# Splits of the next weights behind the root of a norm, and loads of the expert output stage behind its weight loads

## The chip, the cores and the metric

The kernel runs on one core of a Trainium2 chip. The metric is the time of one execution in microseconds (us). Work is spread over TensorE (PE in the profile), VectorE (DVE), ScalarE (ACT) and SyncE (SP), which issues the DMAs from HBM. GpSimd does almost nothing here.

## The reference

Two transformer blocks in a row, on one sequence of 256 tokens with a model width of 1024, all in float32. Cut to what matters here:

```python
# block 1
proj = rmsnorm(h, g_mix) @ w_in                       # mLSTM heads and sliding-window attention
h = h + concat([hm, ha]) @ w_out
h = h + memory_cross_attention(rmsnorm(h, g_cross), rmsnorm(mem, g_mem), ...)
h = h + peer_ffn(rmsnorm(h, g_ffn), w_pq, ..., expert_down, expert_up)
x = rmsnorm(h, g_final)
# block 2, two layers: an even mixer, then an odd one, each followed by an FFN
hn = rms_norm(h, mix_norm_g[layer])
h = h + even_mixer(hn, ...)     # q and k of its first half: rms_norm per head of 64
h = h + conv_ffn(rms_norm(h, ffn_norm_g[layer]), ...)

def rmsnorm(x, g):
    return x * lax.rsqrt(jnp.mean(x * x, axis=-1, keepdims=True) + EPS) * g

def peer_ffn(...):   # per token: 8 heads x 16 of 16384 experts
    a = gelu(expert_down[eidx] . x);  out = sum(g * a * expert_up[eidx])
```

## The kernel before, in words

**Matrix products.** Activations lie transposed, features on the partitions. Each product runs in three passes on a high and a low part of both operands (`mm3`, L439 to L441; `out_step`, L577 to L579 for products that are summed into the residual `h`). So a weight of 128x1024 (512 KB) is handled in four steps: SP loads it into `raw` (L417, `weight`), ACT rounds it into `hi` (L429), DVE subtracts to get `lo` (L430, called the split below), and PE runs 24 matmuls of 256 columns, or 12 of 512 columns, with it. I call that work of PE a piece. There are five weight buffers in the first part of block 1, three in the expert part and six in block 2.

**Norms.** A norm does not hold up the product that follows it. The product runs on `h` times the gain, and the factor 1/rms comes in at the end, in what reads the accumulator. `Norm.columns` (L202) sums the squares on PE into a `tp` bank and calls `rsqrt` (L450): ten dependent DVE operations on 128x2 elements, `rs_m` (L453), `rs_g`, `rs_a` twice, `rs_z`, `rs_a` twice, `rs_p` twice, and the root `rs_y` (L468). `rows` (L218) spreads the root along the tokens: transposes on PE (L213), a copy on ACT (L215) into a tile such as `xR`. `tick` counts pieces: the columns come after the first piece, the rows after the third. `Final` (L256) joins the last norm of block 1 with the first of block 2; its `columns` (L289) run the chain twice, the second time on `fq`, and multiply the two roots (L299). In the even mixer q and k get a norm per head (`head_norm`, L1345), which calls the same `rsqrt` on 128x8 elements, once for each half of the tokens; the transposes of q and k (L1379) wait for it.

**The expert part.** For the experts the kernel computes all of them: 128 weights of `down`, whose outputs go through a gelu and are stored in HBM (`store`, 256 KB for each pair of weights, 55 pairs; the rest stays on the chip), while a gating matrix (`ga`, `gb`) is built. Then the expert output stage runs 128 weights of `up`: for each pair `step` (L1228) reloads the activations (`u`, SP, L1239), multiplies the gate in place (`ga`, DVE, L1240), splits the product (L434, L435) and gives it to `out_step`. A ring of three buffers holds the reloads. The residual `h` (1 MB, from `spill`) and the constants of block 2 (`c_late`, 1.09 MB) are loaded by one DMA each as the stage begins.

**Order.** The code is traced once; a scheduler then puts the instructions of every engine into an order by its own estimate of times, and each engine works in that order. `issue_after(x)` adds the condition that an instruction stands behind `x`. The kernel used it at a few places before, through `gate` in `weight`.

Of the kernel before, what the change touches and what calls it, by code (L numbers as in the profile page):

```python
# [150 lines left out]
class Norm:  # L151
# [50 lines left out]
    def columns(self):  # L202
        ps = self.b.tp()
        self.sums(ps, "s", 0)
        self.r2 = self.b.rsqrt(ps[:, :2], 2, 1.0, keep=self.tag)
        self.r = [self.r2[:, t:t + 1] for t in range(2)]
# [49 lines left out]
class Final(Norm):  # L256
# [32 lines left out]
    def columns(self):  # L289
        b, nc = self.b, self.b.nc  # L290
        ps = b.tp()
        self.sums(ps, "s", 0)
        self.sums(ps, "f", 2)
        self.rf = b.rsqrt(ps[:, :2], 2, 1.0, keep="f")
        q = b.sp.tile([P, 2], F32, tag="fq", name="fq")
        nc.vector.tensor_mul(q, ps[:, 2:4], self.rf)
        nc.vector.tensor_mul(q, q, self.rf)
        r = b.rsqrt(q, 2, 1.0, keep=self.tag)
        nc.vector.tensor_mul(r, r, self.rf)  # L299
        self.r2 = r  # L300
        self.r = [r[:, t:t + 1] for t in range(2)]
# [70 lines left out]
class Builder:  # L372
    def __init__(self, tc, nc, A, out, stages=None):
        self.tc, self.nc, self.A, self.out = tc, nc, A, out
        self.stages = stages
        self.flip = 0
        self.gate = None
        self.free = 100
        self.later = []
        self.mark = None  # L380

# [27 lines left out]
    def weight(self, ap, width=D, parts=1):  # L409
# [6 lines left out]
        for c in cuts:  # L416
            nc.sync.dma_start(raw[:, c], ap[:, c])  # L417
        hi = wp.tile([P, D], F32R, tag="hi", name="hi", bufs=bufs)
        lo = wp.tile([P, D], F32R, tag="lo", name="lo", bufs=bufs)
        with ExitStack() as ctx:  # L420
            if self.gate:
# [4 lines left out]
                if self.free < -4:  # L426
                    self.gate = None
            for c in cuts:
# [21 lines left out]
    def rsqrt(self, ss, n, inv, keep=None):  # L450
# [17 lines left out]
        v.tensor_mul(out, p, z)  # L468
# [144 lines left out]
    def consts(self, names, arr):  # L613
        n = sum(CONST_COLS[k] for k in names)
        t = self.cp.tile([P, n], F32, tag=arr, name=arr)
        self.nc.sync.dma_start(t, self.A[arr])
        o = 0
        for k in names:
            self.c[k] = t[:, o:o + CONST_COLS[k]]
            o += CONST_COLS[k]  # L620

# [455 lines left out]
    def peer(self, xu, base, cw, cx, cq, late, spill, nxt):  # L1077
        nc, A = self.nc, self.A
        mm = nc.tensor.matmul
        with ExitStack() as ctx:  # L1080
# [139 lines left out]
            nc.sync.dma_start(self.h, spill)  # L1220
            self.cp = self.pool(late, "c_late", side="right")
            self.consts(LATE, "c_late")
# [4 lines left out]

            def step(n):  # L1228
                j = order[n // 2]
                if n % 2 == 0:  # L1230
                    if j < GA and cg is not None and "x" not in coef:
# [3 lines left out]
                        self.xq = self.pool(late, "xq2", side="right")  # L1235
                    src = gslice(j, 2)
                    if j < kept:
                        a = acts_next()
                        nc.sync.dma_start(a.rearrange("p i t -> p (i t)"), store[j // 2])  # L1239
                        nc.vector.tensor_mul(src, src, a)  # L1240
# [506 lines left out]
```

## Time and profile before

| | |
|---|---|
| median of 3 runs | 1697.31 us (1692.98 to 1709.5) |
| the profiled execution | 1709.04 us, span 1707.3 us |
| PE busy | 1662.3 us, 97% of the span |
| DVE busy | 1262.0 us, 74% |
| ACT busy | 874.4 us, 51% |
| DMA | 318 MB, mean 186 GB/s |

PE is busy for 97% of the span; 45 us of the span are left. The busy time counts matmuls that run at half clock as well, so it hides a second kind of loss. A share of the whole span says little in such a kernel: what matters is where PE stands still, and what it waits for there.

### The profile page before, as it was taken

What the parts mean: (1) busy time and instruction counts of PE and PEld (TensorE: products, weight loads), DVE (VectorE), ACT (ScalarE), POOL (GpSimd) and SP (SyncE); (2) the same over time, 40 slices, a digit from 0 to 9 for tenths busy, and PEclk for the clock granted to TensorE, in tenths of its full rate; (3) what the DMA queues carried; (4) which work ended last, traced back from release to release, by engine and by line L of the source; (5) the groups of instructions that cost most, each with busy time, mean ns of one, the idle gap of its engine ahead of it and who ended that gap; (6) DMA issues with size and microseconds to landing.
All of it is one profiled execution on the core that took longest, in us unless ns stands there. A gap on an engine that the chain in (4) does not pass through costs nothing.

```text
span 1707.3 us, 33027 instructions
## 1 busy us (share of the span) xinstructions
PE 1662.3 (97%) x13220; PEld 1582.3 (93%) x13220; DVE 1262.0 (74%) x2504; ACT 874.4 (51%) x1358; POOL 0.8 (0%) x11
## 2 busy tenths in 40 slices
PE   7999999999999999999999999899999999999999
PEld 7879899999999999988999999688999997699998
DVE  7686669998798985678655555977777784677775
ACT  6445445545555555444444444655555565455553
POOL 0000000000000000000000000000000000000000
PEclk9999999999999999999999999999999999999999
DMA  8433544577555655889655556543556645345652
GB/s 279 141 104 118 172 166 153 191 230 263 183 195 191 199 193 187 287 291 321 205 186 186 186 186 210 188 138 100 170 190 193 197 151 185 112 155 194 197 192 68
DMA packets 97515, 318.02 MB, mean 186 GB/s; under 512 B 11841, under 2 KB 13505, under 8 KB 96850
## 3 DMA queue, kind: packets, MB, share of 16 engines
q1 hardware_dynamic: 89154, 301.39, 54.2%
q10 hardware_dynamic: 8208, 14.52, 2.2%
q8 instruction: 104, 1.70, 0.4%
q14 instruction: 49, 0.40, 0.1%
HBM read 299.36 MB, written 16.52 MB: 185 GB/s over the span
## 4 chain that ended last, share of the span: by engine, by line
PE 83%; DVE 10%; DMA 4%; issue 2%; ACT 1%; SPq 0%; ACTq 0%; DVEq 0%
PE tp L439 11%; PE tp L441 11%; PE tp L440 11%; PE acc L578 10%; PE acc L579 9%; PE acc L577 9%; PE acc L439 5%; PE acc L440 5%; PE acc L441 5%; DVE lo L430 3%; DMA u<-store 2%; PE tp L1188 1%; PE tp L1189 1%; DMA raw<-w_in_t 1%; ACT hi L429 1%
## 5 line engine op out<-in xcount | busy, mean ns | idle before, releaser
L429 ACT ACTIVATE hi<-raw 128x1024 fp32r<-128x1024 f32 (+1 forms) x533 | 560.6, 1058 | 643.8 <-PE tp L440 247.5
L430 DVE TENSOR_TENSOR lo<-raw,hi 128x1024 fp32r<-128x1024 f32 (+1 forms) x533 | 649.0, 1220 | 295.1 <-ACT hi L429 294.8
L439 PE MATMUL tp<-xh,hi 128*128 128x256 f32 x1680 | 473.2, 282 | 0.4 <-ACT u L1203 0.4
L441 PE MATMUL tp<-xh,lo 128*128 128x256 f32 x1680 | 468.2, 279 | 1.8 <-DVE lo L430 1.8
L440 PE MATMUL tp<-xl,hi 128*128 128x256 f32 x1680 | 467.9, 279 | 0.0
L441 PEld LDWEIGHTS tp<-xh,lo 128*128 128x128 f32 x1680 | 316.6, 188 | 2.2 <-DVE lo L430 2.0
L439 PEld LDWEIGHTS tp<-xh,hi 128*128 128x128 f32 x1680 | 316.8, 189 | 0.6 <-ACT u L1203 0.6
L440 PEld LDWEIGHTS tp<-xl,hi 128*128 128x128 f32 x1680 | 317.0, 189 | 0.0
L578 PE MATMUL acc<-u,hi 128*128 128x256 f32 x1024 | 287.6, 281 | 5.2 <-DVE u L435 5.2
L579 PE MATMUL acc<-u,lo 128*128 128x256 f32 x1024 | 287.4, 281 | 2.3 <-DVE lo L430 2.3
L577 PE MATMUL acc<-u,hi 128*128 128x256 f32 x1024 | 287.1, 280 | 0.0
L578 PEld LDWEIGHTS acc<-u,hi 128*128 128x128 f32 x1024 | 195.4, 191 | 6.1 <-DVE u L435 6.1
L579 PEld LDWEIGHTS acc<-u,lo 128*128 128x128 f32 x1024 | 192.7, 188 | 2.9 <-DVE lo L430 2.9
L577 PEld LDWEIGHTS acc<-u,hi 128*128 128x128 f32 x1024 | 192.3, 188 | 0.0
L439 PE MATMUL acc<-hi,xh 128*128 128x512 f32 (+1 forms) x256 | 101.3, 398 | 6.4 <-ACT y L474 5.8
L440 PE MATMUL acc<-lo,xh 128*128 128x512 f32 (+1 forms) x256 | 100.4, 392 | 0.7 <-DVE lo L430 0.7
L441 PE MATMUL acc<-hi,xl 128*128 128x512 f32 (+1 forms) x256 | 100.0, 391 | 0.0
L577 PE MATMUL acc<-uh,hi 128*128 128x256 f32 x352 | 97.3, 277 | 0.1
L578 PE MATMUL acc<-ul,hi 128*128 128x256 f32 x352 | 97.3, 277 | 0.0
L579 PE MATMUL acc<-uh,lo 128*128 128x256 f32 x352 | 97.1, 276 | 0.0
L577 PE MATMUL acc<-oh,hi 128*128 128x256 f32 x256 | 72.7, 284 | 0.0
L578 PE MATMUL acc<-ol,hi 128*128 128x256 f32 x256 | 71.8, 280 | 0.0
(433 smaller groups left out, 2673.6 us busy)
## 6 DMA issues: line engine op xcount, KB each, us to landing
raw<-down SPq DMA_DIRECT2D x128, 512.0 KB, 3.6
raw<-up SPq DMA_DIRECT2D x128, 512.0 KB, 3.7
raw<-ffn_up SPq DMA_DIRECT2D x88, 512.0 KB, 3.5
raw<-ffn_down SPq DMA_DIRECT2D x44, 512.0 KB, 3.7
raw<-even_in SPq DMA_DIRECT2D x28, 512.0 KB, 4.6
store<-u ACTq DMA_DIRECT2D x55, 256.0 KB, 3.5
u<-store SPq DMA_DIRECT2D x55, 256.0 KB, 4.7
raw<-odd_in SPq DMA_DIRECT2D x24, 512.0 KB, 4.3
```

The lines of the kernel that those rows point to most:

```text
L429: nc.scalar.activation(hi[:, c], raw[:, c], AF.Copy)
L430: nc.vector.tensor_sub(lo[:, c], raw[:, c], hi[:, c].bitcast(F32))
L439: mm(out, lh, rh, start=start, stop=False)
L440: mm(out, lh, rl, start=False, stop=False)
L441: mm(out, ll, rh, start=False, stop=stop)
L577: mm(out, wh[:, cs], oh, start=start and j == 0, stop=False)
L578: mm(out, wh[:, cs], ol, start=False, stop=False)
L579: mm(out, wl[:, cs], oh, start=False, stop=stop and j == 1)
L1188: mm(o, p1[:, b, :, e], hi[:, b, :, e], start=True, stop=False)
L1189: mm(o, p1[:, b, :, e], lo[:, b, :, e], start=False, stop=True)
```

## The change

**The root.** `rsqrt` records its last multiply as `self.root`, whoever calls it; `Final.columns` records the product of its two roots. `columns` sets a counter, `rooted`, to 8, and every `weight` takes one off: from the third to the eighth weight after the columns the `hi` and `lo` of the weight get `issue_after(self.root)`.

**The expert output stage.** A reload is traced four pairs ahead of its use (five pairs at the first step), and stands on SP behind the weight load that was traced last; the multiply of the gate is traced with it. `h` and `c_late` are cut into eight loads each, traced every fourth step from step 48, each behind the last weight load, `c_late` first.

```diff
     def columns(self):                      # Norm
         ...
         self.r2 = self.b.rsqrt(ps[:, :2], 2, 1.0, keep=self.tag)
+        self.b.rooted = 8
...
     def columns(self):                      # Final
         r = b.rsqrt(q, 2, 1.0, keep=self.tag)
-        nc.vector.tensor_mul(r, r, self.rf)
+        b.root = nc.vector.tensor_mul(r, r, self.rf).ins
+        b.rooted = 8
...
     def weight(self, ap, width=D, parts=1):
         for c in cuts:
-            nc.sync.dma_start(raw[:, c], ap[:, c])
+            self.loaded = nc.sync.dma_start(raw[:, c], ap[:, c]).ins
...
+            self.rooted -= 1
+            if 0 <= self.rooted < 6:
+                ctx.enter_context(self.tc.issue_after(self.root))
             for c in cuts:
                 nc.scalar.activation(hi[:, c], raw[:, c], AF.Copy)
                 nc.vector.tensor_sub(lo[:, c], raw[:, c], hi[:, c].bitcast(F32))
...
     def rsqrt(self, ss, n, inv, keep=None):
-        v.tensor_mul(out, p, z)
+        self.root = v.tensor_mul(out, p, z).ins
...
-    def consts(self, names, arr):
+    def consts(self, names, arr, parts=1):
         n = sum(CONST_COLS[k] for k in names)
         t = self.cp.tile([P, n], F32, tag=arr, name=arr)
-        self.nc.sync.dma_start(t, self.A[arr])
+        cuts = [slice(n * i // parts, n * (i + 1) // parts) for i in range(parts)]
+        loads = [lambda c=c: self.nc.sync.dma_start(t[:, c], self.A[arr][:, c]) for c in cuts]
...
             self.h = self.pool(late, "h2", side="right").tile([P, 8, T], F32, tag="h", name="h")
-            nc.sync.dma_start(self.h, spill)
             self.cp = self.pool(late, "c_late", side="right")
-            self.consts(LATE, "c_late")
+            refill = self.consts(LATE, "c_late", 8)
+            refill += [lambda k=k: nc.sync.dma_start(self.h[:, k], spill[:, k]) for k in range(8)]
...
+            def reload(m):
+                if m < len(order) and order[m] < kept:
+                    src = gslice(order[m], 2)
+                    a = acts_next()
+                    with self.tc.issue_after(self.loaded):
+                        nc.sync.dma_start(a.rearrange("p i t -> p (i t)"), store[order[m] // 2])
+                    nc.vector.tensor_mul(src, src, a)
+
             def step(n):
                 j = order[n // 2]
+                if n >= 48 and n % 4 == 0 and refill:
+                    with self.tc.issue_after(self.loaded):
+                        refill.pop(0)()
                 if n % 2 == 0:
...
+                    for m in (range(n // 2 + 4, n // 2 + 5) if n else range(5)):
+                        reload(m)
                     src = gslice(j, 2)
-                    if j < kept:
-                        a = acts_next()
-                        nc.sync.dma_start(a.rearrange("p i t -> p (i t)"), store[j // 2])
-                        nc.vector.tensor_mul(src, src, a)
```

The change moves rows on every engine. The number of instructions stays the same except on SP, where the two loads become 16. Three places show how the order changed; in these rows a name's number is that of its buffer, and the line numbers of the changed kernel are a few higher.

DVE at the norm of the first FFN of block 2, before: the splits stand between the operations of the chain.

```order
L453 TENSOR_SCALAR rs_m_14488<-tp_14485 128x2
L430 TENSOR_TENSOR lo_14596<-raw_14593,hi_14595 128x1024
L455 TENSOR_SCALAR rs_g_14490<-rs_m_14488 128x2
L430 TENSOR_TENSOR lo_14635<-raw_14632,hi_14634 128x1024
L458 TENSOR_TENSOR rs_a_14492<-rs_g_14490 128x2
L430 TENSOR_TENSOR lo_14675<-raw_14672,hi_14674 128x1024
```

The same place in the changed kernel, from the fourth operation before the root on:

```order
L469 TENSOR_TENSOR rs_a_14506<-rs_a_14506,rs_m_14502 128x2
L471 SCALAR_TENSOR_TENSOR rs_p_14513<-rs_a_14506 128x2
L472 TENSOR_SCALAR rs_p_14513<-rs_p_14513 128x2
L474 TENSOR_TENSOR rs_y_14516<-rs_p_14513,rs_z_14509 128x2
L436 TENSOR_TENSOR lo_14610<-raw_14607,hi_14609 128x1024
L436 TENSOR_TENSOR lo_14649<-raw_14646,hi_14648 128x1024
L436 TENSOR_TENSOR lo_14689<-raw_14686,hi_14688 128x1024
L436 TENSOR_TENSOR lo_14723<-raw_14720,hi_14722 128x1024
```

The ten operations of the chain now stand in one run, and the splits behind its root.

PE where block 2 begins, before (`acc_13262` and `acc_13263` are k of the even mixer, `acc_13387` and `acc_13388` its v, `tp_13337` the spread of Final's first root):

```order
L439 MATMUL acc_13263<-hi_13320,xh_12982 128x512
L440 MATMUL acc_13263<-lo_13321,xh_12982 128x512
L441 MATMUL acc_13263<-hi_13320,xl_12983 128x512
L213 MATMUL tp_13337<-ident_92,rs_y_13176 128x128 x2
L439 MATMUL acc_13387<-hi_13391,xh_12982 128x512
L440 MATMUL acc_13387<-lo_13392,xh_12982 128x512
```

The same place in the changed kernel (`acc_13276` and `acc_13277` are k, `acc_13401` and `acc_13402` v, `y_13230` is q of the first half of the tokens, `tp_13421` its transposes):

```order
L447 MATMUL acc_13277<-hi_13280,xl_12997 128x512
L445 MATMUL acc_13276<-hi_13298,xh_12996 128x512
L445 MATMUL acc_13277<-hi_13298,xh_12996 128x512
L214 MATMUL tp_13351<-ident_92,rs_y_13190 128x128 x2
L445 MATMUL acc_13401<-hi_13405,xh_12996 128x512
L445 MATMUL acc_13402<-hi_13405,xh_12996 128x512
L1398 MATMUL tp_13421<-ident_92,y_13230 128x128 x4
L446 MATMUL acc_13276<-lo_13299,xh_12996 128x512
```

And DVE there in the changed kernel (`rs_y_13250` and `rs_y_13273` are the roots of q's head norm for the two halves of the tokens):

```order
L1392 TENSOR_TENSOR y_13230<-y_13230,rs_y_13250 128x512
L474 TENSOR_TENSOR rs_y_13273<-rs_p_13270,rs_z_13266 128x8
L436 TENSOR_TENSOR lo_13299<-raw_13296,hi_13298 128x1024
L1392 TENSOR_TENSOR y_13253<-y_13253,rs_y_13273 128x512
L436 TENSOR_TENSOR lo_13317<-raw_13314,hi_13316 128x1024
L436 TENSOR_TENSOR lo_13335<-raw_13332,hi_13334 128x1024
```

Before, the spread followed the last matmul of k (its eighth piece). Now it stands two matmuls into k's sixth piece, and the third matmul of that piece needs `lo_13299`, which stands behind the root of q's head norm. The splits of v's first three weights stand in the same way behind the root of k's head norm.

SP in the expert output stage, before, a stretch of its first third:

```order
L1239 DMA u2_3256<-store_2516 128x512 x2
L417 DMA raw_9757<-up 128x1024
L1239 DMA u2_3256<-store_2516 128x512
L417 DMA raw_9787<-up 128x1024
L1239 DMA u2_3256<-store_2516 128x512 x2
L417 DMA raw_9821<-up 128x1024
```

and in the changed kernel, a stretch of its second third:

```order
L420 DMA raw_10627<-up 128x1024
L1243 DMA u2_3256<-store_2516 128x512
L420 DMA raw_10661<-up 128x1024
L420 DMA raw_10691<-up 128x1024
L623 DMA c_late_8922<-c_late 128x272
L1243 DMA u2_3256<-store_2516 128x512
L420 DMA raw_10726<-up 128x1024
L420 DMA raw_10756<-up 128x1024
```

Before, three reloads went with every two weights until all 55 were in; now one goes with every two, nearly to the end of the stage, and from the middle on a piece of `c_late` or `h` with every four.

## Rows read from the trace of the kernel before

**Rows 1.** Busy time by stretch: us, PE, PEld, DVE, ACT, POOL, granted clock, DMA.

```profile
99.00:113.00 14.00, 10.93 (x50) 7.88 (x49) 10.67 (x34) 3.65 (x10) 0.00 (x0) 0.76 0.55 186
...
733.00:800.00 67.00, 59.52 (x505) 57.97 (x504) 53.07 (x70) 28.02 (x32) 0.00 (x0) 1.00 0.89 296
800.00:900.00 100.00, 100.00 (x852) 100.00 (x851) 59.97 (x63) 46.64 (x53) 0.00 (x0) 1.00 0.64 211
1086.00:1100.00 14.00, 7.69 (x30) 5.58 (x29) 13.01 (x53) 4.42 (x8) 0.00 (x0) 0.76 0.53 207
1215.00:1225.00 10.00, 6.75 (x45) 6.54 (x44) 8.23 (x20) 3.82 (x8) 0.00 (x0) 0.83 0.82 305
1522.00:1532.00 10.00, 6.74 (x45) 6.54 (x44) 8.12 (x19) 3.98 (x7) 0.00 (x0) 0.83 0.89 320
```

**Rows 2.** What PE waited for, whole span: us in total, times, longest.

```profile
PE tp L213 <- DVE rs_y L468: 8.5, 5, 3.3
...
PE acc L439 <- ACT y L474: 5.8, 1, 5.8
PE acc L578 <- DVE u L435: 5.2, 4, 1.9
```

**Rows 3.** Groups by line, 733 to 800 us: busy us, mean ns, idle before, releaser.

```profile
L1240 DVE TENSOR_TENSOR ga<-ga,u 128x512 f32<-128x512 f32 x35 | 23.5, 687 | 13.9 <-DMA u<-store 13.8
L429 ACT ACTIVATE hi<-raw 128x1024 fp32r<-128x1024 f32 x21 | 22.3, 1063 | 39.0 <-DMA raw<-up 39.0
```

**Rows 4.** Timeline of DVE at the first FFN's norm: start, us, instruction.

```profile
1211.66 0.15 DVE L453 TENSOR_SCALAR rs_m<-tp 128x2 f32<-128x2 f32 x1
1211.73 1.21 DVE L430 TENSOR_TENSOR lo<-raw,hi 128x1024 fp32r<-128x1024 f32 x1
1212.86 0.16 DVE L455 TENSOR_SCALAR rs_g<-rs_m 128x2 int32<-128x2 int32 x1
...
1219.27 0.17 DVE L466 TENSOR_SCALAR rs_p<-rs_p 128x2 f32<-128x2 f32 x1
1219.47 0.16 DVE L468 TENSOR_TENSOR rs_y<-rs_p,rs_z 128x2 f32<-128x2 f32 x1
```

**Rows 5.** Timeline of PE at the same place.

```profile
1216.16 0.28 PE L441 MATMUL acc<-xh,lo 128*128 128x256 f32 x1
1219.69 0.71 PE L213 MATMUL tp<-ident,rs_y 128*128 128x128 f32 x4 [3.25 <-DVE rs_y L468]
...
1221.34 0.41 PE L439 MATMUL tp<-xh,hi 128*128 128x256 f32 x1
1221.55 0.41 PE L440 MATMUL tp<-xl,hi 128*128 128x256 f32 x1
```

**Rows 6.** Timeline of DVE where block 2 begins.

```profile
1077.71 0.16 DVE L453 TENSOR_SCALAR rs_m<-tp 128x2 f32<-128x2 f32 x1 [1.06 <-PE tp L200]
...
1091.14 0.48 DVE L307 SCALAR_TENSOR_TENSOR h<-h,g,fR 128x256 f32<-128x256 f32 x1
...
1093.59 0.75 DVE L476 TENSOR_SCALAR y<-acc,rs_y 128x512 f32<-128x512 f32 x1
...
1098.19 1.29 DVE L1373 TENSOR_TENSOR y<-y,rs_y 128x512 f32<-128x512 f32 x2
```

**Rows 7.** Timeline of PE at the same place.

```profile
1079.00 0.39 PE L439 MATMUL acc<-hi,xh 128*128 128x512 f32 x1
...
1087.79 0.71 PE L213 MATMUL tp<-ident,rs_y 128*128 128x128 f32 x4 [0.39 <-DVE rs_y L468]
1094.33 0.79 PE L439 MATMUL acc<-hi,xh 128*128 128x512 f32 x1 [5.84 <-ACT y L474]
...
1095.35 0.63 PE L441 MATMUL acc<-hi,xl 128*128 128x512 f32 x1
...
1098.46 0.40 PE L441 MATMUL acc<-hi,xl 128*128 128x512 f32 x1
```

**Rows 8.** Timeline of PE at the norm of the memory.

```profile
105.04 1.19 PE L213 MATMUL tp<-ident,rs_y 128*128 128x128 f32 x4 [2.50 <-DVE mx L912]
```

More of the change, by code (lines that the diff above doesn't have):

```diff
@@ L380, in __init__ @@
         self.mark = None
+        self.root, self.rooted = None, 0
     def pool(self, ctx, name, bufs=1, space=None, side=None):
@@ L620, in consts @@
             o += CONST_COLS[k]
+        if parts == 1:
+            loads[0]()
+        return loads
     def masks(self, pool, tmp, *names):
```

## The prediction

> **What bounds the kernel now.** PE does, by its own work: it is busy for 97% of the span, and 45 us are left. So I look for places where PE stands still or runs at half clock, by three views. The busy time of each engine by stretch gives the size of the places [rows 1]: at the norm of the memory 3.1 of 14 us are idle and the granted clock averages 0.76; in the expert output stage 7.5 of 67 us are idle from 733 on and nothing between 800 and 900; where block 2 begins 6.3 of 14, clock 0.76; at the norms of the two FFNs 3.25 of 10 each, clock 0.83. The waits of PE give the names [rows 2]: the root of a norm (8.5 us in five places), y, which is q of the even mixer (5.8 in one), and u, the split product of gate and activations in the expert output stage (5.2 in four). The timelines then show what happens at each.
>
> At the first FFN's norm the chain starts at 1211.66 on DVE and its root is there at 1219.6, though its ten operations take 0.16 us each: a split of 1.13 us stands between them [rows 4]. PE wants to spread the root at 1216.3, stands until 1219.69, and then runs at half pace, 0.21 instead of 0.117 us a matmul [rows 5]; 852 matmuls in 100 us give the 0.117, and 2.8 us for a piece of 24 [rows 1]. The average of 0.83 over 10 us means 3.4 us at the lower level, so 1.7 us lost on top of 3.25. The longer the idle time, the surer the fall: nothing falls in 733 to 800, where the single stops are short.
>
> **The change part by part.**
>
> *Expert output stage.* From 733 to 800 ACT waits 39.0 us for the weights (21 waits) and DVE 13.8 us for reloads [rows 3], with a DMA share of 0.89 at 296 GB/s; from 800 to 900, with fewer reloads, the share is 0.64 at 211 GB/s and PE never stops [rows 1]. The change spreads the reloads: one of 256 KB for every two weights (1024 KB) in 5.6 us is 1.31 MB, 232 GB/s; a piece of h or c_late (131 to 140 KB) for every four weights adds 12. On the line between those two stretches 244 GB/s is a share of 0.74. The gate's multiply comes in time as well: it is traced four pairs, 22 us, ahead, though the ring of three buffers lets a reload land only some two pairs, 11 us, ahead. I take all 7.5 us as gained. Bounds: 0, if the weights still come late, and 7.7 (505 matmuls at 0.117 are 59.3 us). On SP 14 issues are added, at a third of a microsecond each beside an idle queue: nothing. What the weight loads queue behind is one reload, not three.
>
> *The two FFN norms.* Ten operations in a row follow each other every 0.20 us (1219.27 to 1219.47 [rows 4]), so the root is there 2.0 us after 1211.66, at 1213.7, and PE wants it at 1216.3. Four splits queue behind it until 1218.3. The first of them is needed when PE has spread the root and gone on to the next piece, after 1216.3, and is done at 1214.9; each further one takes 1.14 us for a piece of 2.8. So the whole stop goes, and the half clock behind it: 3.25 + 1.7 = 4.95 us, twice 9.9. Bounds: 3.25 each, if some other stop keeps the clock low, and 5.2.
>
> *Memory, cross and expert norm.* At the memory's norm PE stands until 105.04 [rows 8], 3.1 us in all, and the clock of 0.76 over 14 us costs up to 3.3 more [rows 1]. The chain would be through 7 us earlier, but there the splits were needed at once: three of them stand behind the root now, and PE waits for the first of those instead. I take 2.5 us of the 6.4, bounds 0 and 6.4. At the cross norm and the expert norm the waits for the root are what is left of the 8.5: 8.5 - 3.25 - 3.26 - 0.39 (the last one at 1087.79 [rows 7]) = 1.6 us, and all of it goes. The norm at the start and the odd mixer's show no such wait: nothing.
>
> *Where block 2 begins.* Here the change puts a wait in. Before, PE ran the 36 matmuls of pieces 6 to 8 (k) from 1079.0 to 1087.3, 0.23 us each, spread Final's first root at 1087.79, stood until 1094.33 for y, and needed 4.4 us, to 1098.7, for the twelve matmuls of piece 9 (v) instead of 2.8 [rows 7]; the 1.6 between them is the half clock. Meanwhile DVE needed from 1077.71 to 1093.6 for the two chains, because of the splits between them [rows 6]. Now the chains and the residual updates run first. From 1077.71: ten operations (2.0), two of fq (0.4), four of the second chain (0.8) until the spread has come back, then five updates of h with five more operations beside them (0.48 a pair [rows 6], 2.4), hence about 1083.3, less some overlap: I take 1082.7 for the release of y, 10.9 us earlier. But weights 6 to 8 no longer wait for Final's root: `head_norm` overwrites `root` as q is evacuated between the fifth weight and the sixth, and their splits stand behind q's head norm. From the release of y to the end of that root took 1098.19 - 1093.59 = 4.6 us [rows 6]; with the last updates and one multiply ahead of the root, some 6. The split is done at 1082.7 + 6 + 1.14 = 1089.8. PE has two matmuls of piece 6, two of piece 9 and the spread to do until then, to 1081: it stands for 8.8 us. Then 34 matmuls of the pieces 6 to 8 (7.8 us) and the half clock (1.6) bring it to 1099.2. The splits of pieces 9 to 11 stand behind k's head norm, which needs the end of piece 8: 4.6 as for q, one multiply (0.6) and a split (1.14), 6.4 us, to 1105.6. Piece 9 then takes 2.3 and 1.6 for the clock: 1109.5, where it ended at 1098.7 before. Against those 10.8 us some 1.6 us of other matmuls (transposes of q and k, two of piece 12) have been done in the stops. Loss: 9.2 us (10.8 less 1.6). Bounds: 7.5, if the second stop doesn't lower the clock, and 11.5, if the first one lowers it for longer; a gain of 7.9 (6.3 + 1.6), if the waits cost nothing after all.
>
> The rule of the Trainium skill that bears on the chains is in "VectorE: DVE Perf Modes", section "The DRAIN you can't avoid": an operation pays its drain whether or not the next one waits for it, so a dependent chain would run no slower than a mixed one. These rows differ: a chained operation follows after 0.20 us [rows 4], where the one ahead of a split lets it start 0.07 us later. By the rule, with 0.16 for 0.20, some thirty chained operations where block 2 begins would be 1.2 us shorter, the loss 8.0, and the sum below 13.5 where it says 12.3.
>
> *Sum.* 7.5 + 9.9 + 2.5 + 1.6 - 9.2 = 12.3 us less. The profiled execution took 1709.04 us (1.7 around its span), so 1696.7; it lay 11.7 us above the median of 1697.31, at the top of the three runs. Nothing in the sum depends on that difference, so against the median: 1685.0 us, 0.7% less. 1% (17 us) is about what a measurement of this kernel can tell from no change.
>
> **The rivals.** *All norms gain.* The scheduler's order would have to be harmless where block 2 begins: DVE reaches q's head norm before PE runs dry. Then its 7.9 us come on top: 7.5 + 9.9 + 2.5 + 1.6 + 7.9 = 29.4 less, 1667.9. For it: DVE stands idle or does only prefetching splits in that stretch. Against it: q's head norm needs Final's root, and the order leaves PE four matmuls in the meantime.
>
> *The expert stage gains nothing.* The loads of the weights stay late, because DMAs and not their order were the limit: 12.3 - 7.5 = 4.8 less, 1692.5. For it: 0.89 is nearly full, and the same bytes move. Against it: the same kernel moved 211 GB/s right after without a stop.
>
> *Slower.* One mechanism, in the expert stage: the multiplies of the gate now stand among the splits for the whole stage, and DVE works in order, so a late reload holds the splits of two weights. Per pair DVE has two splits (2.3 us), a multiply and half of the u split (1.3 to 2): about 3.9 of 5.6 us. A reload that keeps it waiting for more than 1.7 us in every pair stops PE; over the 35 reloads from 733 to 800 the wait came to 13.8 us, 0.4 a reload [rows 3]. If it were 2.2 in each, 55 x 0.5 = 27 us: 1697.3 + 27.5 - 4.8 = 1720. "DMA: Bandwidth & Descriptors" in the Trainium skill, section "Rules for kernel authors", speaks for it, as it asks for 1 MiB and more a transfer and the change cuts two such loads into pieces of an eighth; the trace before has no load of that size beside these weights to show it.
>
> **How the numbers follow.** The forecast has 0.55; all norms gain 0.17; the expert stage gains nothing 0.18; slower 0.10. The range reaches from 1668 (the first rival) to 1699 (the second rival with the larger loss of 11.5 and 0 at the memory's norm: 1692.5 + 2.3 + 2.5 = 1697.3, and a little for the runs). Faster by over 1% is below 1680.3: the first rival, and the forecast where the memory's norm gives all of its 6.4 and the loss is 7.5 (12.3 + 3.9 + 1.7 = 17.9), a third of its chance: 0.17 + 0.18 = 0.35. Slower by over 1%: 0.09 of the last rival. The rest, 0.56, lies within 1%.
>
> **What would show it.** In the changed kernel's timeline: PE without a stop in the expert output stage, and no wait of DVE for a reload above 1.7 us; the roots of the FFN norms 2.0 us behind the start of their chains, and PE's spread without a wait; where block 2 begins two stops of PE, 8.8 and 6.4 us, both released by a split behind a head norm. The prediction is wrong if the second of these stops isn't there, or if the weights come late between 800 and 1050 us.

## The result: slower by 0.7%, and where the time went

| | median of 18 runs | lowest to highest |
|---|---|---|
| before | 1701.27 us | 1692.98 to 1716.91 |
| changed kernel | 1714.59 us | 1702.85 to 1722.15 |

The ratio is 1.0067, with an interval of 1.0045 to 1.0088: some 11 us slower. That is within the 1% of the prediction's middle case, but the interval does not reach 1, the time lies above the range, and the sign is the other one. The profiled execution of the changed kernel took 1714.27 us, span 1712.5. Its windows, in the columns of [rows 1] (us, PE, PEld, DVE, ACT, POOL, granted clock, DMA). The first is moved by 6 us to 93, as the sums of the memory's norm come at 87.1 here and at 92.6 before; 900 to 1000 is new, and where block 2 begins is left to its timeline below, as it comes 7 us earlier here:

```profile
93.00:107.00 14.00, 11.92 (x75) 10.17 (x74) 12.23 (x34) 5.69 (x18) 0.00 (x0) 0.88 0.45 152
733.00:800.00 67.00, 63.08 (x542) 61.70 (x541) 39.37 (x46) 29.20 (x34) 0.00 (x0) 1.00 0.65 227
800.00:900.00 100.00, 95.88 (x831) 94.51 (x830) 62.70 (x70) 45.66 (x52) 0.00 (x0) 1.00 0.67 235
900.00:1000.00 100.00, 98.10 (x858) 97.29 (x857) 62.79 (x70) 46.47 (x55) 0.00 (x0) 1.00 0.73 247
1215.00:1225.00 10.00, 10.00 (x89) 10.00 (x89) 9.69 (x23) 7.29 (x11) 0.00 (x0) 1.00 0.71 220
1522.00:1532.00 10.00, 9.98 (x87) 9.78 (x86) 9.69 (x20) 7.94 (x11) 0.00 (x0) 1.00 0.57 190
```

The two FFN norms are mended: 89 and 87 matmuls where there were 45, and a granted clock of 1.00. The memory's norm is mended in part: 2.1 us idle for 3.1, a clock of 0.88 for 0.76, and the stop that is left waits for a split behind the root:

```profile
96.26 0.39 PE L447 MATMUL acc<-uh,lo 128*128 128x256 f32 x1 [2.01 <-DVE lo L436]
```

In the expert output stage the stops of the beginning are fewer (63.1 us busy for 59.5), but now they go on in every stretch: 4.1 us idle from 800 to 900, 1.9 in the next 100, where PE never stopped before. And in 900 to 1000 there is an oddity: PE is idle for 1.9 us, and yet got through 858 matmuls, where 852 filled 100 us before [rows 1]. That is taken up under "Two paces".

**The expert output stage.** Waits of the changed kernel from 733 to 1060 us (in total, times, longest):

```profile
DVE ga L1244 <- DMA u<-store: 107.2, 50, 3.6
ACT hi L435 <- DMA raw<-up: 91.6, 44, 3.9
...
PE acc L584 <- DVE u L441: 8.1, 14, 1.2
```

DVE waits for nearly every reload, 2.1 us each (107.2 / 50). Its timeline there, and after it SP's (start, us, instruction):

```profile
909.22 0.69 DVE L441 TENSOR_TENSOR u<-ga,u 128x512 fp32r<-128x512 f32 x1
911.25 0.69 DVE L1244 TENSOR_TENSOR ga<-ga,u 128x512 f32<-128x512 f32 x1 [1.34 <-DMA u<-store]
911.86 1.22 DVE L436 TENSOR_TENSOR lo<-raw,hi 128x1024 fp32r<-128x1024 f32 x1
914.55 0.69 DVE L1244 TENSOR_TENSOR ga<-ga,u 128x512 f32<-128x512 f32 x1 [1.48 <-DMA u<-store]
915.16 1.22 DVE L436 TENSOR_TENSOR lo<-raw,hi 128x1024 fp32r<-128x1024 f32 x1
```

```profile
906.72 0.42 SPq L1243 DMA_DIRECT2D u<-store  x1
907.60 2.07 SPq L420 DMA_DIRECT2D raw<-up  x2
909.72 0.43 SPq L1243 DMA_DIRECT2D u<-store  x1
913.10 0.33 SPq L420 DMA_DIRECT2D raw<-up  x1
```

And what SP's queue waited for from 690 to 1060 us:

```profile
SPq L420 <- DVE lo L436: 268.7, 124, 5.0
```

The reload is issued at 906.72 and the multiply can start at 911.25, 4.5 us later; the next pair, 909.72 and 914.55, has 4.8. In DVE's order each multiply stands close behind the issue of its load: DVE comes to it some 3.2 us after the issue (911.25 less its wait of 1.34), before the load has landed. DVE works in order, so the split at 911.86 waits with it; SP waits for the splits to free a weight buffer (124 waits); so the next weights are loaded late (91.6 us of ACT's waiting), and PE stops for the split product. The DMAs have room: a share of 0.65 to 0.73.

**The first FFN's norm.** DVE, then PE (the answers to [rows 4, 5]):

```profile
1214.92 0.15 DVE L459 TENSOR_SCALAR rs_m<-tp 128x2 f32<-128x2 f32 x1
...
1216.69 0.16 DVE L474 TENSOR_TENSOR rs_y<-rs_p,rs_z 128x2 f32<-128x2 f32 x1
1216.77 2.36 DVE L436 TENSOR_TENSOR lo<-raw,hi 128x1024 fp32r<-128x1024 f32 x2
```

```profile
1219.03 0.28 PE L445 MATMUL acc<-xh,hi 128*128 128x256 f32 x1
1219.14 0.28 PE L446 MATMUL acc<-xl,hi 128*128 128x256 f32 x1
1219.25 0.28 PE L447 MATMUL acc<-xh,lo 128*128 128x256 f32 x1
1219.37 0.60 PE L214 MATMUL tp<-ident,rs_y 128*128 128x128 f32 x4
...
1220.16 0.28 PE L445 MATMUL tp<-xh,hi 128*128 128x256 f32 x1
1220.28 0.28 PE L446 MATMUL tp<-xl,hi 128*128 128x256 f32 x1
1220.40 0.28 PE L447 MATMUL tp<-xh,lo 128*128 128x256 f32 x1
```

The chain takes 1.9 us with nothing between its operations, the splits follow, and PE spreads the root without a wait. Ahead of the spread the matmuls start every 0.113 us, behind it every 0.118.

**Where block 2 begins.** DVE, then PE:

```profile
1070.42 0.16 DVE L459 TENSOR_SCALAR rs_m<-tp 128x2 f32<-128x2 f32 x1 [2.49 <-PE tp L200]
...
1081.21 0.69 DVE L1392 TENSOR_TENSOR y<-y,rs_y 128x512 f32<-128x512 f32 x1
1081.82 0.16 DVE L474 TENSOR_TENSOR rs_y<-rs_p,rs_z 128x8 f32<-128x8 f32 x1
1081.90 1.22 DVE L436 TENSOR_TENSOR lo<-raw,hi 128x1024 fp32r<-128x1024 f32 x1
```

```profile
1072.41 0.71 PE L214 MATMUL tp<-ident,rs_y 128*128 128x128 f32 x4
1076.77 1.20 PE L445 MATMUL acc<-hi,xh 128*128 128x512 f32 x2 [3.64 <-ACT y L480]
1081.96 1.12 PE L1398 MATMUL tp<-ident,y 128*128 128x128 f32 x4 [4.00 <-DVE y L1392]
1083.17 0.79 PE L446 MATMUL acc<-lo,xh 128*128 128x512 f32 x1
...
1086.75 0.59 PE L446 MATMUL acc<-lo,xh 128*128 128x512 f32 x1
...
1098.70 1.12 PE L1398 MATMUL tp<-ident,y 128*128 128x128 f32 x4 [3.85 <-DVE y L1392]
```

The old wait for y is there still, shorter (3.64 for 5.84 [rows 7]), and two new stops stand behind it, 4.00 and 3.85 us, one at the head norm of q and one at that of k. After the first, PE runs at half clock until 1086.75 or so.

**Two paces.** The granted clock is 1.00 on both sides of the spread at 1219.37, and still the 256-column matmuls follow each other every 113.3 ns on one side and every 117.8 on the other. All traces of this study show these two paces. One holds for tens to hundreds of microseconds and changes only where PE's stream is broken: at a stop, at transposes, at sums, at a rise of the clock. And one kernel takes different ones in different executions. The middle of the first FFN in two executions of the kernel before, the one shown so far first:

```profile
1240.00:1380.00 140.00, 140.00 (x1238) 140.00 (x1237) 104.45 (x156) 73.16 (x103) 0.00 (x0) 1.00 0.61 194
```

```profile
1240.00:1380.00 140.00, 140.00 (x1191) 140.00 (x1191) 99.93 (x150) 71.00 (x100) 0.00 (x0) 1.00 0.57 186
```

The difference is 4.5 ns a matmul. For the 3072 matmuls of the expert output stage it is 13.7 us, for an FFN some 6, as much as the terms in dispute. So stages are compared below at equal pace: from the length of the expert output stage I take 13.7 us times the share of its matmuls that ran at 118 (counted from the starts of successive matmuls in PE's timeline). Stages are cut at the sums of squares of the norms. The repeats are e1 and e12 (before) and e5, e11 and e15 (changed).

| profiled execution | block 1 to expert norm | expert output (share at 118) | the same at equal pace | even mixer | FFN 0 (pace) | FFN 1 (pace) |
|---|---|---|---|---|---|---|
| before | 245.4 | 383.0 (87%) | 371.1 | 134.2 | 187.0 (113) | 189.1 (113) |
| before, second | 244.0 | 383.3 (87%) | 371.4 | 134.7 | 194.4 (118) | 193.8 (118) |
| before, third | 244.3 | 380.3 (90%) | 368.0 | 134.4 | 187.1 (113) | 195.3 (118) |
| changed | 238.8 | 383.0 (13%) | 381.2 | 144.7 | 188.0 (118) | 190.1 (118) |
| changed, second | 239.8 | 381.6 (25%) | 378.2 | 145.8 | 188.0 (118) | 184.0 (113) |
| changed, third | 238.3 | 385.7 (56%) | 378.0 | 144.6 | 181.9 (113) | 190.2 (118) |
| changed, fourth | 239.4 | 383.9 (35%) | 379.1 | 145.8 | 181.9 (113) | 190.2 (118) |

The expert part ahead of the output stage (447.4 to 449.7) and the odd mixer (120.5 in all seven) did not change.

The column at equal pace takes the pace for a plain addition, and for the changed stage it is not. e14 below has that stage unchanged, and ran 74% of it at 118. It took 380.5 us, 370.3 at equal pace: as much as before. Its waits from 733 to 1060 us:

```profile
DVE ga L1244 <- DMA u<-store: 104.3, 51, 3.7
...
ACT hi L435 <- DMA raw<-up: 63.8, 31, 3.7
...
PE acc L584 <- DVE u L441: 3.7, 7, 1.3
```

DVE waits for the reloads as long as in the changed kernel, but ACT waits less for the weights, and PE stops half as often for the split product. At 118 a pair of weights (48 matmuls) takes PE 0.22 us longer, so up to that much more of a wait is covered; over 55 pairs that is 12 us, an estimate from the two paces. Compared as measured: with the reloads of before, the stage took 370.4, 371.9, 372.9 and 373.4 us where it ran at 113 for 80 to 90% (e2, e4, e7, e8), and 380.3 to 383.3 where it ran at 118 for as much. With the reloads of the change it took 380.5 to 385.7 at every share from 13 to 74%. So against the stage of before, which has stops of its own, the change of the stage cost some 8 to 13 us at the faster pace, and nothing that can be seen at the slower one. The 8.9 us below are a mean over traces of mixed pace.

### The profile page after: what moved, and what is told of

Read it like the earlier page. It is cut to its first block, busy times and chain, and to the rows that moved or that the text cites. A ratio compares the mean times of both kernels' runs of the same rounds, so it can differ in the third digit from the quotient of the medians.

```text
span 1712.5 us, 32980 instructions
## 1 busy us (share of the span) xinstructions
PE 1668.3 (97%) x13220; PEld 1584.7 (93%) x13220; DVE 1259.9 (74%) x2504; ACT 873.7 (51%) x1358; POOL 0.8 (0%) x11
## 4 chain that ended last, share of the span: by engine, by line
PE 76%; DVE 12%; DMA 8%; ACT 2%; issue 1%; SPq 1%; DVEq 0%; ACTq 0%
PE tp L445 11%; PE tp L447 11%; PE tp L446 11%; PE acc L584 7%; PE acc L585 7%; PE acc L583 7%; DMA u<-store 6%; PE acc L447 5%; PE acc L446 5%; DVE lo L436 5%; PE acc L445 5%; ACT hi L435 1%; PE tp L1198 1%; PE tp L1199 1%; DMA raw<-up 1%
## 5 line engine op out<-in xcount | busy, mean ns | idle before, releaser
L584 PE MATMUL acc<-u,hi 128*128 128x256 f32 x1024 | 285.3, 279 | 8.2 <-DVE u L441 8.1
L585 PE MATMUL acc<-u,lo 128*128 128x256 f32 x1024 | 283.9, 277 | 2.3 <-DVE lo L436 2.3
L583 PE MATMUL acc<-u,hi 128*128 128x256 f32 x1024 | 283.4, 277 | 0.0
L1244 DVE TENSOR_TENSOR ga<-ga,u 128x512 f32<-128x512 f32 x52 | 36.0, 692 | 111.4 <-DMA u<-store 111.4
```

The lines of the kernel that those rows point to most:

```text
L583: mm(out, wh[:, cs], oh, start=start and j == 0, stop=False)
L584: mm(out, wh[:, cs], ol, start=False, stop=False)
L585: mm(out, wl[:, cs], oh, start=False, stop=stop and j == 1)
```

## The experiments

Each ratio is to runs of the kernel before that were timed together with it; intervals are 95%. e2, e3 and e4 were timed together, as were e6 to e8, e9 and e10, and e13 to e15.

| run | ratio to before | what it is |
|---|---|---|
| e2_roots_only | 0.9939 [0.9918, 0.9960] | the root part alone |
| e3_stage_only | 1.0022 [0.9999, 1.0045] | the expert stage's part alone |
| e4_own_root | 0.9881 [0.9859, 0.9903] | the root part, each norm with its own root |
| e6_late_multiply | 0.9999 [0.9968, 1.0030] | the stage's part, multiply one pair ahead |
| e7_pieces_only | 0.9985 [0.9953, 1.0017] | only the loads in eight pieces |
| e8_spread_again | 0.9926 [0.9893, 0.9959] | e4, one more transpose in the spread |
| e9_both_mended | 0.9905 [0.9870, 0.9939] | changed kernel, own root and late multiply |
| e10_after_own_root | 0.9963 [0.9932, 0.9993] | changed kernel, own root |
| e13_after_late | 1.0003 [0.9982, 1.0024] | changed kernel, late multiply |
| e14_after_spread | 1.0040 [1.0010, 1.0070] | changed kernel, one more transpose |
| e15_after_fourth | 1.0043 [1.0018, 1.0067] | changed kernel, nothing else |

**The two parts apart.** The root part alone keeps the reloads, `h` and `c_late` of before; the stage part alone takes out the condition.

Against the changed kernel, e2's stage and then e3's condition:

```diff
-                    for m in (range(n // 2 + 4, n // 2 + 5) if n else range(5)):
-                        reload(m)
+                    if j < kept:
+                        a = acts_next()
+                        nc.sync.dma_start(a.rearrange("p i t -> p (i t)"), store[j // 2])
+                        nc.vector.tensor_mul(src, src, a)
```

```diff
-            if 0 <= self.rooted < 6:
-                ctx.enter_context(self.tc.issue_after(self.root))
```

> The splits behind the root alone, the expert output stage as before. Theory P: in both FFNs PE's stop goes and the pace falls to 117.8, so each stage from an FFN's norm on is no faster than before (0 to 2 us slower); where block 2 begins some 10.5 us are lost as in the changed kernel; the norms of block 1 give back some 5: 1.000 to 1.006 of before. Rival Q (the pace is chance, the stops are what counts, as predicted): the FFNs give 9.9 us, block 2's begin costs 9 to 10.5, block 1 gives 4 to 6: 0.995 to 0.998. Rival R (the loss of the changed kernel comes from the expert output stage): below 0.997.

> The expert output stage as in the changed kernel, no split behind a root. Theory P: DVE waits for reloads for some 100 us and PE stops there for some 10 us in all, as in the changed kernel, at the fast pace; the stage takes within 2 us of before's if that has the slow pace (trace of before) and up to 10 us more than before's where that has the fast one; the FFNs have the stop and the fast pace; 0.998 to 1.006. Rival (prediction: reloads in time): no stops in the stage, 0.995.

The roots alone gain 10 us; the median lies where rival R had it, below the ranges of theory P and rival Q. The stage alone loses some 4, with an interval that just takes in no change, where the prediction had 7.5 gained. The two don't add up: together they would give 0.996, and the changed kernel has 1.0067 and 1.0043, 14 to 18 us more. That is taken up under "What picks the pace". In e3's trace DVE waits for reloads 107.4 us in 52 waits with the norms as before, so the waits belong to this part. Its expert output stage takes 380.9 us, 44% of it at 118: 374.9 at equal pace, 4.7 more than the mean of before (370.2).

**The overwritten root.** Only a norm's own columns set the root; the head norms don't.

```diff
         self.r2 = self.b.rsqrt(ps[:, :2], 2, 1.0, keep=self.tag)
+        self.b.root = self.b.last
...
-        self.root = v.tensor_mul(out, p, z).ins
+        self.last = v.tensor_mul(out, p, z).ins
```

> The splits behind the root, but the root is taken in the norm's columns alone, so the head norms don't overwrite it; expert output stage as before. Both theories: where block 2 begins PE stops once, some 3 us, for a split behind Final's root, instead of 5.8 in before and two stops in the changed kernel: 4 to 6 us less than before there, some 14 us less than with the overwritten root. Theory P: FFNs no faster: 0.990 to 0.997 of before. Rival Q: the FFNs give 9.9 on top: 0.986 to 0.990.

> The changed kernel with the root taken in the norm's columns alone; the expert output stage as changed, with its waits for reloads. If the loss of the changed kernel is the overwritten root (12 to 13 us where block 2 begins) and the expert output stage (8 to 11 us at equal pace): 12 to 13 us less than the changed kernel, 0.998 to 1.002 of before, and 12 to 20 us more than with both mended. If the two parts disturb each other in some other way: far from this sum.

Both gain against the kernel with the same stage and the overwritten root: e4 against e2 0.58% of 1705.6, 9.9 us; e10 against the changed kernel 0.8 to 1.0%, 14 to 18 us, though the two were not timed together. The 0.9963 of e10 is below what was expected. The even mixer takes 133.1 us in e4 and 145.2 in e2. What is left in e4 of PE's stops there is the wait for y alone:

```profile
1064.09 0.71 PE L215 MATMUL tp<-ident,rs_y 128*128 128x128 f32 x4
1068.45 0.80 PE L446 MATMUL acc<-hi,xh 128*128 128x512 f32 x1 [3.65 <-ACT y L481]
```

The profiled execution of e10 had a granted clock of 0.95 over the whole span, so its stages are not compared. e4 is the best version of the study.

**The multiply one pair ahead.** The loads are traced where e3 has them; the multiply is traced one pair ahead of its use, not four, behind the last split.

```diff
             def reload(m):
...
-                    nc.vector.tensor_mul(src, src, a)
+            def multiply(m):
+                if m in ring:
+                    src = gslice(order[m], 2)
+                    with self.tc.issue_after(self.parted):
+                        nc.vector.tensor_mul(src, src, ring.pop(m))
...
+                    for m in range(n // 2 + 1 if n else 0, n // 2 + 2):
+                        multiply(m)
```

> The expert output stage alone, with the gate's multiply moved: the reload is issued as early as in the changed kernel, its multiply stands one pair ahead of its use, behind the split traced last, where the changed kernel has it right behind the reload's issue. Theory W (a reload takes some 5 us to land, DVE comes to its multiply 3 us after the issue, waits, and holds the splits behind it, and by them the next weight loads): the wait of DVE for reloads falls from 107 us to under 15, and PE's stops in the stage from 12 to under 4 us; at the same pace the stage takes 8 to 10 us less than with the stage alone, 370 us at the fast pace and 381 at the slow one. Rival D (the DMAs are too slow for the mixed load, the waits only show it): waits of ACT for weights take the place, stops of 8 us and more stay.

> The changed kernel with the gate's multiply one pair ahead of its use, the root still overwritten. If the late reloads cost the changed kernel what the traces say at equal pace (379 against 361 to 362 us in the stage, 17 to 18 us): 0.990 of the changed kernel, 0.996 of before. If this stage then takes the slow pace, as in both traces of kernels with the late multiply (374.7 and 375.9): 383 - 375 = 8 us less, 0.995 of the changed kernel, 1.001 of before.

The stage's window in e6 and then in the changed kernel:

```profile
733.00:1050.00 317.00, 317.00 (x2694) 317.00 (x2693) 204.05 (x226) 147.80 (x168) 0.00 (x0) 1.00 0.72 237
```

```profile
733.00:1050.00 317.00, 306.48 (x2653) 302.33 (x2652) 195.54 (x220) 143.67 (x165) 0.00 (x0) 1.00 0.68 233
```

And DVE's waits in e6 there:

```profile
DVE lo L434 <- ACT hi L433: 112.0, 112, 1.6
```

PE never stops, no wait for a reload is left, and the DMAs move more, not less. So it was the place of the multiply and not the loads. The medians bear it out: where only the place of the multiply differs, e9 is 10.2 us below e10 and e13 7.8 us below e15. But e6 runs the whole stage at 118: 2694 matmuls in 317 us are 117.7 ns each. It takes 374.7 us, 361.0 at equal pace, 9 less than before, whose traces ran at nearly the same pace; e9 and e13 show the same (375.9 and 374.1, both 100%). The stages with stops, when they ran at 113 for most of the time, were a little quicker: 370.4 in e2 and 371.9 in e4, both with the old loads. That fits the median of e6, which is level with before.

**The pieces alone.** `h` and `c_late` in eight loads each; the condition on the root and `reload` are out, and `step` reloads as before.

```diff
-                    for m in (range(n // 2 + 4, n // 2 + 5) if n else range(5)):
-                        reload(m)
+                    if j < kept:
+                        a = acts_next()
+                        nc.sync.dma_start(a.rearrange("p i t -> p (i t)"), store[j // 2])
+                        nc.vector.tensor_mul(src, src, a)
```

> The reloads as before, in a burst; only h and c_late are cut into eight loads each and put between the weight loads from step 48 on. Theory W: the burst is 2.1 MB lighter, so the stops of before (9.6 us in eight) get a little less, 5 to 9 us; no stop where the pieces are loaded; 0.995 to 1.001 of before, by the pace. Rival D (the small loads hold up the weights): stops behind the pieces, 1.002 or more.

No cost can be seen: 0.9985. The Trainium skill, "DMA: Bandwidth & Descriptors", section "Rules for kernel authors", asks for 1 MiB and more a transfer where the most bandwidth is wanted. With pieces of an eighth this run shows no loss, at a DMA share of 0.62 to 0.68 from 800 to 1000 us, so here the measurement decides against what the prediction made of the rule.

**Both mended.** Own root and late multiply in the changed kernel, its diff the sum of the two above.

> The changed kernel with both faults mended: the root taken in the norm's columns alone, and the gate's multiply one pair ahead of its use. If the terms add at equal pace (expert output stage 8 to 9 us less than before, the FFNs 10, block 1 some 4, the begin of block 2 some 2): 24 us less, 0.986 of before; by the pace alone 0.980 to 0.992. Stages whatever the pace: FFNs 181.9 and 184.1 (fast) or 188 and 190 (slow), expert output stage 362 (fast) or 375 (slow). If the gains are given back by a slower pace as a rule: 0.993 or more.

0.9905, level with e4 (0.9881) within the intervals: with the waits gone the stage's part neither gains nor loses anything that can be measured. The 0.986 of the terms added at equal pace was not reached.

**What picks the pace.** Unchanged kernels were profiled again, and the spread of a root got a third transpose, as its break lies between the paces at the FFN.

```diff
-        for t in range(2):
+        for t in (0, 0, 1):
```

> As with the root of the norm's own columns, and at each spread PE does the transposes of the first half of the tokens a second time (the same values), two more passes of 0.11 us at nine places, 2 us in all. Theory P: the pace behind the spread of an FFN's norm depends on what PE did in the break; in twelve spreads of six traces the pace always changed from the one to the other there. With another length of the break it may stay: then both FFNs are at the slow pace where the kernel without it has the fast one, 6 us each, 1.006 of that kernel. Rival (the pace hangs on something outside of PE's stream, as where buffers lie): the same pace as without, and 1.001.

> The changed kernel, with the first transposes of each spread done twice (2 us in all at most). If the break at the spread sets the FFNs' pace and the longer break leads to the fast one (as in the one trace with it, from either pace ahead of it): both FFNs 182 and 184 us, some 6 to 9 us less than the changed kernel on the average, which had the slow pace in four of six FFNs: 0.995 of it. If the break doesn't matter: 1.001 of it, and FFNs at either pace.

> The kernel before, unchanged, a second trace. In the two traces matmuls of 256 columns follow each other at one of two paces, 113.3 or 117.8 ns, for tens to hundreds of us; before had the slow one from 798 to 1062 us and the fast one in both FFNs, the changed kernel the other way round. Theory P (the pace is set anew at each break of PE's stream and then stays): the stretches may differ from the first trace of before where a stop ends a little differently, above all after the last stop of the expert output stage, and the time differs by 4.45 ns for each matmul that changed its pace, up to some 10 us in that stage. Rival (the pace belongs to the code of a stage): the same stretches as in the first trace, and a stage differs by less than 1 us.

> The changed kernel, unchanged, a second trace. In its first trace both FFNs ran at 117.8 ns a matmul (188.0 and 190.1 us from norm to norm), with the splits behind the root alone both ran at 113.3 (181.9 and 184.1) with the same instructions on PE there. Theory P (what PE's pace is after a break depends on how it enters the break, and is the same for a kernel in most executions): slow in both FFNs again, some 1714 us. If the pace is drawn anew in each execution: fast in both about every second time, then some 1702 us. Either way both FFNs have the same pace as each other, and the expert output stage has its stops again, within 2 us of 383.

> The changed kernel, a third trace, for its pace: stages of 362 + stops and the like can be compared only at equal pace. In two traces three of four FFNs were slow and the expert output stage mostly fast. Expected: 381 to 383 us with 14 to 16 us of stops in the expert output stage if it is fast again, up to 394 if slow; each FFN 182 to 184 or 188 to 190.

> The kernel before, a third trace, for its pace. Expected: each FFN 187 to 189 or 194; the expert output stage 371 (fast) to 383 (slow) with some 9 us of stops either way. If the fast pace in this stage is frequent for this kernel, that explains why its median of 1701 to 1705 us lies below its two traces so far (1709 and 1721).

> The changed kernel once more, timed beside the two others: 1.005 to 1.009 of before. In its trace: 1709 to 1715 us; if the pace explains the spread of its runs, a slow FFN costs 6 us more than a fast one and the expert output stage up to 13.7, and a trace below 1705 us has both FFNs fast and this stage mostly fast.

e8 had both FFNs at 113, as e2, e4 and e9 have without the added transpose, and e14 both at 118: the added transpose decides nothing, and that theory fell. The ratio of e8 lies 0.45% above that of e4, more than its 2 us of transposes; the two were not timed together, and this stays open. So did the theories that the pace belongs to the code of a stage (before had both FFNs at 113 in its first trace and at 118 in its second) and that both FFNs of an execution share it (changed, second: 188.0 and 184.0). e15's ratio, 1.0043, lies below the 1.005 to 1.009 that was expected. In the repeats the FFNs of the changed kernel ran at 118 in 5 of 8, those of before in 3 of 6. What picks the pace stays open.

One pattern was seen only afterwards. The six traces with one part of the change or a piece of it (e2, e3, e4, e6, e7, e8) have all twelve FFNs at 113; those with both parts (the changed kernel four times, e9, e13, e14) have 5 of 14. At 6 us for an FFN at 118 that is some 8 us an execution (9 / 14 x 2 x 6, an estimate), and the change of the stage costs most at the 113 pace. Together these could account for the 14 to 18 us by which the two parts don't add up; no run shows that they do.

## Why the prediction was wrong, point by point

**The step that failed: the expert output stage.** "The gate's multiply comes in time as well" stood behind the 7.5 us. At equal pace the stage went from a mean of 370.2 to one of 379.1: 8.9 us more where the prediction took 7.5 off, so this term missed by 16.4. (The mean hides the pace: some 8 to 13 us at 113, none seen at 118.) The loads were traced four pairs ahead, and I took the time that a load has to land from that distance, as if the multiply stood near the use of its pair. But the multiply was traced with the load, and DVE came to it 3.2 us after the issue, where the load took 4.5 to 4.8 us to land. The weights came late between 800 and 1050 us, which the prediction had named as a sign that it is wrong. The rival "Slower" named the mechanism and its threshold, 1.7 us a pair; the waits were 2.1. Its price of 27 us was too high, since it made a stop of the whole excess in each pair: PE's stops of over 0.25 us in this stage came to 14.1 to 15.9 us in the four traces, for 6.6 to 9.9 in the three of before. That is some 6 of the 8.9 us; the other 2 to 3 lie in no stop that I could name. In e14, at the slower pace, the same waits leave stops of some 7.5 us, as before. The rival had a chance of 0.10. That the DMAs were the limit ("the expert stage gains nothing") is refuted: at 237 GB/s and a share of 0.72 e6 has no stop. Its time is not: the median of e6 is level with before.

**FFN norms.** Right. 4.95 us each were predicted. At the 113 pace FFN 0 went from 187.0 and 187.1 to 181.9 twice, FFN 1 from 189.1 to 184.0: 5.1 each. At 118 the gains are 6.4 and 3.6 to 5.2. Without the condition FFN 0 took 185.4 to 188.0 at the 113 pace in all such traces (e3, e6 and e7 besides), so the gain there is 3.5 to 6.1. The chained operations follow each other every 0.20 us (1214.92 to 1216.69 in nine steps), as the prediction took them.

**Memory, cross and expert norm.** Right in mechanism: at the memory's norm PE stands 2.0 us for the first split behind the root, and the spreads of the cross and the expert norm have no wait. 4.1 us were predicted, 5.5 found in the changed kernel (from a mean of 244.6 to one of 239.1). Six other traces with the same condition (e2, e4, e8, e9, e13, e14) took 241.5 to 243.7, 0.9 to 3.1 less than that mean, so the size is known only to a few us.

**Where block 2 begins.** Right in mechanism, and e4 shows that the overwritten root is the cause. The sum came near, 9.2 predicted and 10.8 found (from a mean of 134.4 to one of 145.2). DVE kept to the forecast: the split that PE needs is done 12.6 us after the chain's start (1070.42 to some 1083.0), for 12.1 predicted. But I had the wait for y gone, and let PE do its two matmuls of v before; they wait for y. So the first stop, 8.8 us in the forecast, is there in two parts, 3.64 and 4.00. At k the stop was 3.85 us for 6.4. PE stood less than forecast, and the loss is still larger by 1.6 us; what makes up for it was not taken apart, so the nearness of the sum is in part luck. The half clock behind the first stop came as forecast (a granted clock of 0.68 from 1082 to 1090 us). The stops end at the multiply by the root of the head norm (y), as the transposes of q and k stand ahead of the matmul that needs the split. The rival "all norms gain" expected 7.9 us from the wait for y going away; in e4, where the head norms hold no split, 3.65 us of it stay, and the even mixer is 1.3 us shorter than before, not 7.9.

**The sum.** At equal pace, with the mean of 8.9 for the stage: 8.9 - 10.2 - 5.5 + 10.8 = 4.0 us slower, where -12.3 was forecast; of the miss of 16.3 the expert stage makes up all. The runs without a profile say 11 us in the first measurement (1.0067) and 7 in e15 (1.0043). The rest, 3 to 7 us, is not shown. The pace could account for it: the profiled executions of before (1709.0, 1721.5, 1713.5) all lie above its medians of 1701 to 1706, all with some 88% of the expert stage at 118, so the others may have run it at 113 more often, while the changed kernel's profiled ones (1714.3, 1710.9, 1710.4, 1712.8) lie at or below its medians of 1714.6 and 1713.4. With the reloads of before the stage took some 10 us less at 113 than at 118, and with those of the change it took no less. But the pace of an execution without a profile can't be seen, and this stays open. For the same reason e6's 9 us at equal pace stand beside a ratio of 0.9999.

## What to carry to other kernels

A prefetch is early only if its consumer stands late: when an engine works in order, look at what is queued behind the instruction that reads the loaded tile, and put that instruction one step ahead of its use, not right behind the issue of the load. A mark such as "the last root" that every caller of a helper overwrites becomes a dependence on the wrong event; let the caller that means it set it. And before stages of two profiled executions are compared, compare the distance of successive matmuls in them, and run the old kernel again. In a stage where PE waits, the slower pace hides part of the waits, and can't be taken off as a plain addition.

## What was not expected of the hardware

PE has two paces at a granted clock of 1.00, 113.3 and 117.8 ns between 256-column matmuls, 4% of the time of the stages concerned, and the same kernel takes either in different executions. The stage without stops ran at 117.8 throughout in each of e6, e9 and e13, so the end of all stops brought nothing over a stage that stops for 6 to 8 us and runs at 113. And one execution of e10 had a granted clock of 0.95 throughout, though its time (1710.35) is no more than 0.7% above the median of that kernel, and its matmuls followed each other every 118 ns or so where others of a clock of 1.00 do too (425 in 50 us from 850 on).
